# Half-size weight loads, free stage distances, full-height compressed values and unused products at the start of a two-layer hybrid decoder

## Chip, cores and metric

The kernel runs on one core of one Trainium2 chip. The metric is the device time of one execution in microseconds (us). The kernel before took 648.5 us (median of three runs, 647.51 to 649.08).

## What is computed

A trunk of two pre-norm residual layers on 256 tokens of width 1024, all in float32. In every layer four token mixers with four heads of 64 each read one normalised input through one input projection of 2956 columns. Their outputs go through one output projection, and an MLP with squared ReLU (width 4096) follows. A last RMS norm ends it. Cut to what matters:

```python
for layer in range(2):
    h = _rmsnorm(x, norm_attn[layer])
    proj = h @ w_in[layer]                       # 1024 x 2956
    o_sb = stick_breaking_attention(...)         # "sb"
    o_mb = moba_attention(...)                   # "mb", one 256-block here: causal softmax with bias
    o_ns = nsa_attention(...)                    # "ns": g0 * compressed + g1 * selected + g2 * window
    o_df = diff_attention(...)                   # "df": softmax1 - lam * softmax2, then RMS norm
    x = x + concat(o_sb, o_mb, o_ns, o_df) @ w_out[layer]
    h2 = _rmsnorm(x, norm_mlp[layer])
    x = x + square(relu(h2 @ w_up[layer])) @ w_down[layer]
return _rmsnorm(x, final_norm)
```

The compressed branch of "ns" first makes 15 compressed keys and values from windows of 32 tokens: a product of 2048 x 256 weights (w1), a GELU, and a second product (w2). With 256 tokens every selected block is causal, so the selected and the window branch have the same scores up to keys and values.

## The kernel before

**Products.** Every product with a weight is made of three, because each float32 operand is split into a rounded part (hi) and the rest (lo): hi*hi, hi*lo, lo*hi. A piece of weights is loaded by SP's queue (tile `wraw`, 1 MB, three buffers), split by ACT into `whi` (a copy that rounds) and by DVE into `wlo` (a subtraction), in halves of 0.5 MB with four buffers each, and then streamed by TensorE. `class Weights` (lines 631 to 656) holds this: `load` starts the load, `part(i)` makes the split of half i. The first group of the projection ("vg", 396 columns) has smaller pieces (792 KB).

**Stages.** The start loads x, normalises it, transposes it on TensorE into `x` (hi and lo). The projection runs group by group: "vg" (values, gates), "sqk" (queries and keys of sb), "nqk" (of ns), "dqk" (of df), "v2" (values of df and mb), "mqk" (of mb). Queries and keys are split (`qth`, `qtl`), and then restacked by loads from one place of SBUF to another (`stack2`, tile `s`; `stack3` goes through DRAM, tile `st`), which run on SP's queue too. Each head of a mixer is a unit (lines 857, 905, 960, 1068) that gives up control between its stages: scores, softmax, transposes, product with the values. `compress` (line 1004) makes the compressed keys `KC` and values `VC`, reading `wraw` straight as a moving operand with stationary tiles of 32 columns. Then follow the output projection and the MLP, which are nearly all weight products.

**What sets the order.** No engine's order is written down. Calls are recorded with a due time: `at(clock, offset)` sets it, `run` (line 848) takes a head's first due time from the table `START` and adds a constant `STAGE` of 1.2 for each further stage, `LOADS` says how long ahead of its use a piece is loaded, and `LEADS` the same for its split. `Order.schedule` (line 348) then places call after call on the five engines, always the ready one of the earliest due time whose buffers are free; `choose` (line 360) passes over calls that can't start, but on SP it stops at the first load that has no buffer. It has constants for the engines' costs (`GAP`, `DRAIN` and others). The order it makes is fixed in the program; on the chip each engine works through its own list and waits on semaphores. Loads use eight semaphores in turn, so in the program a load waits until the eighth load ahead of it has landed.

**The small set-up.** `setup_consts`, `setup_bias` and `setup_small` (lines 562 to 626) load masks, the table of the relative bias (`tb`, `hot`, `rt`; one product `ps<-t,tb` on TensorE, a trip through DRAM, and six copies to `Bt` on DVE) and small vectors. They stand between the projections of layer 0.

Of the kernel before, what the change touches and what calls it, by code (L numbers as in the profile page):

```python
# [27 lines left out]
    "sb": ((-2128.1, -135.2, -1435.8, 37.9), (-286.7, -731.7, -641.4, 39.7)),  # L28
    "ns": ((27.1, -1051.7, 53.8, 45.5), (48.2, -2101.2, 32.8, -175.5)),
    "cw": ((-1062.2,), (-2120.7,)),  # L30
    "cmp": ((-1801.8,), (-695.1,)),
    "df": ((-1887.0, -3174.2, -1854.8, -2205.7), (24.0, -2246.5, 53.7, 52.7)),
    "mb": ((-87.3, -1433.6, -45.1, -356.5), (-276.0, -1568.2, -350.0, -7140.8)),
# [9 lines left out]
)  # L43
LEADS = (
# [17 lines left out]
)  # L62
CW_LOAD = 41.5
STAGE = 1.2

FIRST = (-100.5, -617.1)
# [63 lines left out]
GAP, DRAIN = 13.0, 94.0  # L130
# [5 lines left out]
SPARE = {"ps": 2}  # L136

# [40 lines left out]
class Order:  # L178
# [169 lines left out]
    def schedule(self):  # L348
# [11 lines left out]
        def choose(e):  # L360
            skipped, pick = [], None
            while ready[e] and pick is None:
# [121 lines left out]
def trunk(ctx: ExitStack, tc: tile.TileContext, x, w_in, w_out, w_up, w_down, gattn, gains, pos, cw1, cw2,  # L484
# [50 lines left out]
    nc.sync.dma_start(gn, gains)  # L535
    for f in range(2):
# [9 lines left out]
    negone = cp.tile([128, 128], F32R, name="negone")  # L546
    nc.gpsimd.memset(F(negone), -1.0)
# [5 lines left out]
    KC = [cp.tile([128, 2, 16], F32R, name=f"KC{i}") for i in range(2)]  # L553
    w2 = cp.tile([128, DEPTH, 2, 2, 64], F32, name="w2")
# [7 lines left out]
    def setup_consts():  # L562
# [4 lines left out]
        for i in range(2):  # L567
            nc.gpsimd.tensor_copy(KC[i], Pc[:, 0, 0, :].rearrange("p (a b) -> p a b", a=2))
        for l in range(DEPTH):
# [11 lines left out]
    def setup_bias():  # L581
# [5 lines left out]
        nc.sync.dma_start(rt, rows)  # L587
        p = ps_att()
# [4 lines left out]
        nc.sync.dma_start(scr, vb[:12])  # L593
        for g in range(6):
# [6 lines left out]
            nc.vector.tensor_copy(Bt[:, 2 * g:2 * g + 2, :], rev)  # L601
        nc.gpsimd.memset(Bc, 8.0 * NEG)
# [3 lines left out]
    def setup_small():  # L606
        lv = t2()
        nc.sync.dma_start(lv[:, :DEPTH * 128], lamv.to_broadcast([128, DEPTH * 128]))
        d = small(4)
# [12 lines left out]
        sl = small(2)  # L622
        nc.sync.dma_start(sl, subln)
# [7 lines left out]
    class Weights:  # L631


        def __init__(self, src, n, parts):
            self.src, self.n, self.m, self.raw = src, n, n // parts, None
            self.k = n_piece[0]
            n_piece[0] += 1

        def load(self, clock):
            if self.raw is None:  # L640
                at(clock, -LOADS[self.k])
                self.raw = wp.tile([128, 2048], F32, name="wraw", tag="wraw", bufs=3)
                nc.sync.dma_start(self.raw[:, :self.n], self.src)
                at(clock)
            return self.raw

        def part(self, i, clock):
            self.load(clock)
# [3 lines left out]
            src = self.raw[:, i * self.m:(i + 1) * self.m]  # L652
# [78 lines left out]
    def proj(l, name, xT, tok, clock):  # L731
# [6 lines left out]
        ws = [Weights(w_in[l, :, o + i * 4 * n:o + (i + 1) * 4 * n], 4 * n, 2) for i in range(2)]  # L738
# [109 lines left out]
    def run(unit, l, name, h):  # L848
# [3 lines left out]
        for _ in unit(h):  # L852
            clock += STAGE
            at(clock)
# [149 lines left out]
    def compress(l, clock, early):  # L1004
# [4 lines left out]
        for i in range(2):  # L1009
            w = [Weights(cw1[l, kv, :, i * 2048:i * 2048 + 2048], 2048, 1) for kv in range(2)]  # L1010
            w = [a.load(early + 1.8 * i) for a in w]
            at(clock)
            for j in range(4):
                for kv in range(2):
                    for m in range(2):
                        g, ic = 32 * (2 * kv + m), 2 * j + m
                        x0 = 256 * kv + 16 * (8 * i + ic)
                        mm(acc[g:g + 32, :256], xf[:, x0:x0 + 32], w[kv][:, ic * 256:(ic + 1) * 256],
# [368 lines left out]
```

## Time and profile before

| | |
|---|---|
| median of 3 runs | 648.5 us |
| profiled execution | 648.43 us |
| its span, first to last instruction | 646.7 us |
| TensorE (PE) busy | 622.2 us, 96% |
| VectorE (DVE) busy | 441.7 us, 68% |
| ScalarE (ACT) busy | 358.9 us, 56% |
| GpSimd (POOL) busy | 8.3 us, 1% |
| moved by loads and stores | 126.94 MB, mean 196 GB/s |
| chain that ended last | PE 75%, DMA 9%, DVE 8%, ACT 5% |

All calls carry line 480, where the recorded calls are issued, so rows are told apart by tiles. In a row, `out<-in` are tiles without their numbers, `PEld` is TensorE's load of a stationary tile, `SPq` an issue on SP's queue. A matmul's time in a row reaches from its start to its modelled end, and matmuls overlap: the spacing of their starts says how fast TensorE goes. The time outside the span (648.43 less 646.7) is 1.7 us.

### The profile page before, as it was taken

The numbers are of one execution on the slowest core, as the hardware profiler recorded it, in microseconds if no ns is written. First come the engines' busy times: TensorE is split into PE (matmuls) and PEld (weight loads), VectorE is DVE, ScalarE is ACT, GpSimd is POOL, SyncE is SP. The second block draws the span as 40 slices with busy tenths as digits, with TensorE's granted clock in tenths as the row PEclk, the third lists the DMA queues.
The fourth block names the chain that finished last, engine by engine and source line by source line (L and its number), as shares of the span: only waits on it lengthen the run. The fifth ranks groups of instructions, "written<-read, shape, count | busy, mean of one in ns | idle before, by whom it ended". The sixth has DMA issues, their size and how long they took to land.

```text
span 646.7 us, 9744 instructions
## 1 busy us (share of the span) xinstructions
PE 622.2 (96%) x3674; PEld 529.0 (82%) x3674; DVE 441.7 (68%) x900; ACT 358.9 (56%) x693; POOL 8.3 (1%) x25
## 2 busy tenths in 40 slices
PE   5989999999999999999999999999999999999995
PEld 4978768788888888888889977887788888888885
DVE  5749579779576566556686674998866666576466
ACT  5547587566455454445364774776744454454453
POOL 2010000000000000000000000000000000000000
PEclk9999999999999999999999999999999999999999
DMA  7787955844354465555636958446355555545531
GB/s 275 254 246 227 273 196 222 255 148 176 122 215 155 176 256 186 199 192 196 212 112 222 276 222 235 190 126 236 127 196 195 196 199 191 197 162 196 196 130 66
DMA packets 26895, 126.94 MB, mean 196 GB/s; under 512 B 3880, under 2 KB 5928, under 8 KB 14048
## 3 DMA queue, kind: packets, MB, share of 16 engines
q1 hardware_dynamic: 26848, 126.32, 57.0%
q8 instruction: 29, 0.48, 0.3%
q14 instruction: 18, 0.15, 0.1%
HBM read 115.79 MB, written 3.17 MB: 184 GB/s over the span
## 4 chain that ended last, share of the span: by engine, by line
PE 75%; DMA 9%; DVE 8%; ACT 5%; issue 1%; SPq 1%; POOLq 0%; POOL 0%; ACTq 0%; DVEq 0%
PE ps L480 75%; DMA wraw<-in_w_in_dram 3%; DVE wlo L480 3%; DVE t L480 2%; ACT t L480 2%; ACT whi L480 2%; DMA wraw<-in_cw_dram 2%; DVE xs L480 1%; DMA cst<-in_cst_dram 1%; DMA s<-qtl 1%; DMA wraw<-in_w_down_dram 1%; DVE x L480 1%; SPq L480 1%; DMA t<-bias_scratch 1%; ACT x L480 1%
## 5 line engine op out<-in xcount | busy, mean ns | idle before, releaser
L480 DVE TENSOR_TENSOR wlo<-wraw,whi 128x1024 fp32r<-128x1024 f32 (+1 forms) x192 | 231.2, 1212 | 109.6 <-ACT whi L480 93.7
L480 ACT ACTIVATE whi<-wraw 128x1024 fp32r<-128x1024 f32 (+1 forms) x192 | 199.8, 1049 | 147.0 <-PE ps L480 111.3
L480 PE MATMUL ps<-x,whi 128*128 128x256 f32 (+1 forms) x1024 | 212.7, 341 | 0.7 <-DVE x L480 0.7
L480 PEld LDWEIGHTS ps<-x,whi 128*128 128x128 f32 x1024 | 153.8, 190 | 15.9 <-issue 1.2
L480 PE MATMUL ps<-whi,t 128*128 128x512 f32 (+1 forms) x528 | 162.6, 385 | 0.3 <-ACT whi L480 0.3
L480 PEld LDWEIGHTS ps<-x,wlo 128*128 128x128 f32 x768 | 112.9, 190 | 12.0 <-issue 0.6
L480 PE MATMUL ps<-x,wlo 128*128 128x256 f32 x768 | 122.0, 283 | 0.1
L480 PEld LDWEIGHTS ps<-whi,t 128*128 128x128 f32 x528 | 97.8, 188 | 20.1 <-ACT whi L480 1.0
L480 PE MATMUL ps<-wlo,t 128*128 128x512 f32 (+1 forms) x264 | 101.0, 385 | 0.0
L480 ACT ACTIVATE t<-ps 128x256 f32<-128x256 f32 (+1 forms) x109 | 44.1, 413 | 45.9 <-PE ps L480 45.1
L480 PEld LDWEIGHTS ps<-wlo,t 128*128 128x128 f32 x264 | 49.7, 188 | 9.5 <-DVE wlo L480 0.2
L480 ACT ACTIVATE t<-t 128x512 fp32r<-128x512 f32 (+5 forms) x53 | 29.3, 552 | 35.4 <-DVE t L480 33.6
L480 ACT ACTIVATE t<-t,sm 128x128 f32<-128x128 f32 (+1 forms) x98 | 42.2, 443 | 10.7 <-DVE sm L480 10.4
L480 DVE TENSOR_TENSOR t<-ps,t 128x256 f32<-128x256 f32 x64 | 26.7, 421 | 28.0 <-ACT t L480 27.3
L480 PE MATMUL ps<-whi,x 128*128 128x512 f32 (+1 forms) x128 | 36.0, 384 | 1.0 <-ACT x L480 1.0
L480 DVE TENSOR_TENSOR t<-t,t 128x512 fp32r<-128x512 f32 (+2 forms) x44 | 27.4, 622 | 8.0 <-ACT t L480 6.9
L480 DVE CUSTOM_DVE_ANT_0 t<-ps,Bt 128x256 f32<-128x256 f32 (+1 forms) x80 | 24.4, 352 | 9.0 <-PE ps L480 9.0
L480 PEld LDWEIGHTS ps<-whi,x 128*128 128x128 f32 x128 | 23.1, 193 | 4.7 <-ACT x L480 1.5
L480 PE MATMUL ps<-whi,mixh 128*128 128x512 f32 (+1 forms) x68 | 26.7, 397 | 0.0
L480 PE MATMUL ps<-whi,mixl 128*128 128x512 f32 (+1 forms) x68 | 26.5, 389 | 0.0
L480 PE MATMUL ps<-wlo,mixh 128*128 128x512 f32 (+1 forms) x68 | 26.3, 386 | 0.0
L480 DVE SCALAR_TENSOR_TENSOR t<-t 128x512 f32<-128x512 f32 (+1 forms) x36 | 22.9, 635 | 1.0
(139 smaller groups left out, 475.1 us busy)
## 6 DMA issues: line engine op xcount, KB each, us to landing
wraw<-in_w_up_dram SPq DMA_DIRECT2D x32, 1024.0 KB, 4.8
wraw<-in_w_down_dram SPq DMA_DIRECT2D x32, 1024.0 KB, 4.8
wraw<-in_w_in_dram SPq DMA_DIRECT2D x20, 1024.0 KB, 4.9
wraw<-in_cw_dram SPq DMA_DIRECT2D x8, 1024.0 KB, 9.4
wraw<-in_w_out_dram SPq DMA_DIRECT2D x8, 1024.0 KB, 6.6
s<-qth SPq DMA_DIRECT2D x28, 128.0 KB, 4.3
s<-qtl SPq DMA_DIRECT2D x28, 128.0 KB, 3.2
wraw<-in_w_in_dram SPq DMA_DIRECT2D x4, 792.0 KB, 6.7
```

What stands on the lines that cost most here:

```text
L480: fn(*a, **k)
```

## The change

Five things change in the code, and with them all tables of due times.

1. A piece of weights is loaded in two halves of 0.5 MB (396 KB in "vg"), each with its own tile: six buffers of 128x1024 in place of three of 128x2048, and a due time in `LOADS` for each half. `compress` takes its weights in halves too.
2. `run` takes the distance from each stage to the next out of a table `STAGES`, by mixer, layer, head and stage, in place of the constant 1.2. The set-up calls get due times of their own (`SETUP`).
3. `VC` becomes one constant tile of 128 rows by four heads; head h fills only its own 32 rows, the others stay zero. The product with the values then takes all 128 rows of `PcT`, in place of a 32-row tile of the array.
4. Forty products of a constant tile with itself, whose result nothing reads, stand ahead of the first transposes on TensorE; the tile they read is now the first that POOL fills.
5. `choose` lets SP pass over up to four loads that have no buffer; `GAP` goes from 13 to 14.

```diff
-LOADS = (
-    73.4, 61.3, 61.1, 82.6, 43.8, 72.8, 7.3, 8.2, 12.4, 12.9, 12.9, 2.7, 12.4, 54.6, 14.0, 10.8, 14.3, 8.1, 7.0,
...
+LOADS = (
+    (60.0, 60.0), (43.4, 52.4), (31.5, 52.8), (53.2, -1.0), (-1.0, 2.0), (11.9, -1.0), (-1.0, 60.0), (3.1, 7.5),
...
-STAGE = 1.2
+STAGES = {
+    "sb": (((-4.1, -139.2, -205.8, 69.1, 218.6), (-250.0, 90.5, -244.3, 66.4, -11.9), (-90.8, 226.5, -190.8,
...
-GAP, DRAIN = 13.0, 94.0
+GAP, DRAIN = 14.0, 94.0
...
+WARM = 40
...
-                    if e == "SP":
+                    if e == "SP" and len(skipped) == 4:
                         skipped.append(x)
                         break
...
+    at(-1000.0)
+    negone = cp.tile([128, 128], F32R, name="negone")
+    nc.gpsimd.memset(F(negone), -1.0)
...
+    at(-1000.0)
+    p = ps_att()
+    for i in range(WARM):
+        mm(p[:, 0:128], negone, negone, i == 0, i == WARM - 1)
+    at(-100.0)
...
+    VC = cp.tile([128, 4, 64], F32, name="VC")
+    nc.gpsimd.memset(VC, 0.0)
...
-        def load(self, clock):
-            if self.raw is None:
-                at(clock, -LOADS[self.k])
-                self.raw = wp.tile([128, 2048], F32, name="wraw", tag="wraw", bufs=3)
-                nc.sync.dma_start(self.raw[:, :self.n], self.src)
+        def load(self, i, clock):
+            if self.raw[i] is None:
+                at(clock, -LOADS[self.k][i])
+                self.raw[i] = wp.tile([128, 1024], F32, name="wraw", tag="wraw", bufs=6)
+                nc.sync.dma_start(self.raw[i][:, :self.m], self.src[:, i * self.m:(i + 1) * self.m])
...
-        for _ in unit(h):
-            clock += STAGE
+        for s, _ in enumerate(unit(h)):
+            clock += STAGES[name][l][h][s]
             at(clock)
...
-        VC = ap.tile([128, 64], F32, name="VC", tag="VC", bufs=2)
-        evac(VC, p[:, 0:64])
-        return VC, clock
+        for h in range(4):
+            r = slice(32 * h, 32 * h + 32)
+            evac(VC[r, h], p[r, 0:64])
+        return clock
...
-            av.append((VCs[0][32 * h:32 * h + 32], PcT[32 * h:32 * h + 32], 0))
+            av.append((VC[:, h], PcT, 0))
```

The order that comes out is another one almost everywhere. Three places follow.

SP's queue at the start, before: x, the first two pieces of "vg" and those of the groups behind it (`wraw_111`, `wraw_116` are "vg"; `wraw_123`, `wraw_128` "sqk"), and the small loads of the set-up behind them.

```order
L480 DMA xs_68<-in_x_dram 128x512 x2
L480 DMA ident_69<-in_eye_dram 128x128
L480 DMA gains_70<-in_gains_dram 128x24
L480 DMA xs_68<-in_x_dram 128x512 x2
L480 DMA wraw_111<-in_w_in_dram 128x1584
L480 DMA wraw_128<-in_w_in_dram 128x2048
L480 DMA wraw_116<-in_w_in_dram 128x1584
L480 DMA wraw_123<-in_w_in_dram 128x2048
L480 DMA wraw_188<-in_w_in_dram 128x2048
L480 DMA wraw_183<-in_w_in_dram 128x2048
L480 DMA wraw_298<-in_w_in_dram 128x2048
L480 DMA cst_71<-in_cst_dram 128x547
```

And with the change, from the fourth half of a weight on (all of x, `ident`, `gains` and three halves of "vg" stand ahead; `wraw_119` is the last half of "vg", `wraw_127` the first half that "sqk" needs, `wraw_130` and `wraw_133` its next two).

```order
L511 DMA wraw_130<-in_w_in_dram 128x1024
L511 DMA wraw_119<-in_w_in_dram 128x792
L511 DMA wraw_133<-in_w_in_dram 128x1024
L511 DMA tb_176<-in_table_dram 32x12
L511 DMA t2_177<-in_hot_dram 32x512
L511 DMA rt_178<-in_rows_dram 12x513
L511 DMA cst_71<-in_cst_dram 128x547
L511 DMA pst_85<-in_pos_dram 128x32
L511 DMA w2_83<-in_cw2_dram 128x256
L511 DMA wraw_217<-in_w_in_dram 128x1024
L511 DMA pst_85<-in_pos_dram 128x32
L511 DMA wraw_127<-in_w_in_dram 128x1024
```

The loads of the bias table moved ahead of the weights of the second group, and the first half of that group went behind nine other loads.

TensorE around the product of the bias table (`ps<-t,tb`), before, in the middle of the third group's products (`x_101,whi` and `x_101,wlo`):

```order
L480 MATMUL ps<-x_101,whi 128x256 x16
L480 MATMUL ps<-x_101,wlo 128x256 x8
L480 MATMUL ps<-x_101,whi 128x256 x2
L480 MATMUL ps<-t_171,tb 12x512
L480 MATMUL ps<-x_101,whi 128x256 x14
```

And with the change, where `whi,x_103` with 396 columns is "vg" and `x_103,whi` is the second group:

```order
L511 MATMUL ps<-whi,x_103 128x396 x5
L511 MATMUL ps<-wlo,x_103 128x396 x2
L511 MATMUL ps<-whi,x_103 128x396 x2
L511 MATMUL ps<-t_177,tb 12x512
L511 MATMUL ps<-x_103,whi 128x256 x16
```

It moved up by one group, to the end of "vg".

TensorE around the product of the compressed values (`PcT,VC`) in layer 0, before; `64x256` and `64x128` are the products with the values, which use half the array's columns, and `whi,mixh` is the output projection:

```order
L480 MATMUL ps<-whi,mixl 128x512
L480 MATMUL ps<-PcT,VC 64x256 x2
L480 MATMUL ps<-ident,t_270 128x128 x3
L480 MATMUL ps<-ident,t_271 128x128 x3
L480 MATMUL ps<-whi,mixh 128x512
```

And with the change, later in the same layer:

```order
L511 MATMUL ps<-t_289,Vn 64x256
L511 MATMUL ps<-t_300,Vn 64x256
L511 MATMUL ps<-t_289,Vn 64x128
L511 MATMUL ps<-t_300,Vn 64x128
L511 MATMUL ps<-PcT,VC 64x256 x2
L511 MATMUL ps<-t_327,V_318 64x256
```

The product stands among others of its own array shape.

## Rows read from the trace of the kernel before

**Rows 1.** The page, parts 1 and 2: busy time by engine, load share and GB/s in 40 slices.
```profile
PE 622.2 (96%) x3674; PEld 529.0 (82%) x3674; DVE 441.7 (68%) x900; ACT 358.9 (56%) x693; POOL 8.3 (1%) x25
DMA  7787955844354465555636958446355555545531
GB/s 275 254 246 227 273 196 222 255 148 176 122 215 155 176 256 186 199 192 196 212 112 222 276 222 235 190 126 236 127 196 195 196 199 191 197 162 196 196 130 66
```

**Rows 2.** Windows of 20 us: length, then busy PE, PEld, DVE, ACT, POOL; clock; DMA share, GB/s.
```profile
20.00:40.00 20.00, 18.98 (x149) 17.95 (x148) 11.39 (x15) 8.90 (x14) 2.57 (x6) 1.00 0.86 272
...
180.00:200.00 20.00, 20.00 (x105) 16.68 (x104) 13.31 (x17) 10.09 (x15) 0.00 (x0) 1.00 0.53 192
```

**Rows 3.** Timeline of PE at the start: start us, us, what, count, idle before and releaser.
```profile
7.41 4.17 PE L480 MATMUL ps<-ident,xn 128*128 128x128 f32 x16 [7.41 <-DVE xn L480]
...
12.97 0.86 PE L480 MATMUL ps<-whi,x 128*128 128x396 f32 x2
13.63 0.66 PE L480 MATMUL ps<-wlo,x 128*128 128x396 f32 x2
...
18.80 0.52 PE L480 MATMUL ps<-wlo,x 128*128 128x396 f32 x2
19.16 0.34 PE L480 MATMUL ps<-whi,x 128*128 128x396 f32 x1
```

**Rows 4.** Timeline of ACT and of DVE at the start, the splits of "vg".
```profile
10.21 1.62 ACT L480 ACTIVATE whi<-wraw 128x792 fp32r<-128x792 f32 x2 [1.03 <-DMA wraw<-in_w_in_dram]
...
18.16 2.11 DVE L480 TENSOR_TENSOR wlo<-wraw,whi 128x792 fp32r<-128x792 f32 x2
```

**Rows 5.** Timeline of PE, 34 to 46 us: the bias product and the first scores.
```profile
34.25 1.01 PE L480 MATMUL ps<-t,tb 32*12 32x512 f32 x2 [1.02 <-DMA t<-in_hot_dram]
...
45.52 0.68 PE L480 MATMUL ps<-s,s 128*128 128x256 f32 x4 [1.07 <-DMA s<-qtl]
```

**Rows 6.** Timeline of SP's queue: the restacking of "sb" in layer 0, first and last issues.
```profile
33.64 2.45 SPq L480 DMA_DIRECT2D s<-qth  x4
...
41.39 2.00 SPq L480 DMA_DIRECT2D s<-qtl  x2
```

**Rows 7.** Timeline of PE in layer 0: "ns" scores and compression weights.
```profile
61.74 0.47 PE L480 MATMUL ps<-nkh,s 128*128 128x512 f32 x1 [0.27 <-DMA s<-qtl]
...
71.87 1.93 PE L480 MATMUL ps<-wraw,XF 128*32 128x256 f32 x32 [0.63 <-DMA wraw<-in_cw_dram]
73.73 0.87 PE L480 MATMUL ps<-t,Vn 128*64 128x256 f32 x8
```

**Rows 8.** Timeline of PE in layer 1: scores of "sb", "ns" and "mb", compression.
```profile
361.04 1.12 PE L480 MATMUL ps<-x,wlo 128*128 128x256 f32 x8
362.00 0.57 PE L480 MATMUL ps<-s,s 128*128 128x256 f32 x4
...
372.44 0.94 PE L480 MATMUL ps<-nkh,s 128*128 128x512 f32 x4 [1.04 <-ACT t L480]
...
398.59 1.72 PE L480 MATMUL ps<-wraw,XF 128*32 128x256 f32 x28 [0.69 <-DMA wraw<-in_cw_dram]
...
438.86 0.47 PE L480 MATMUL ps<-s,s 128*128 128x256 f32 x2 [1.27 <-DMA s<-qtl]
```

**Rows 9.** Timeline of PE: two of one array shape, then a change of shape.
```profile
119.71 0.40 PE L480 MATMUL ps<-wlo,mixh 128*128 128x512 f32 x1
119.94 0.40 PE L480 MATMUL ps<-whi,mixl 128*128 128x512 f32 x1
120.27 1.52 PE L480 MATMUL ps<-t,Vn 128*64 128x256 f32 x16
```

**Rows 10.** Waits of TensorE's weight loads and of SP's queue: us in total, times, longest.
```profile
PEld ps L480 <- issue: 12.2, 36, 1.7
...
SPq L480 <- DMA wraw<-in_w_in_dram: 24.5, 8, 5.3
```

**Rows 11.** Loads from one tensor: KB each, median us from issue to landing.
```profile
wraw<-in_w_in_dram SPq DMA_DIRECT2D x20, 1024.0 KB, 4.9
```

More of the change, by code (lines that the diff above doesn't have):

```diff
@@ L27 @@
 START = {
[L28 to L33, printed above, removed]
+    "sb": ((-0.7, 25.9, -122.8, 41.4), (-194.1, -250.0, -250.0, 49.9)),
+    "ns": ((-37.7, -235.8, 48.9, 58.0), (30.4, -206.6, -244.7, -55.9)),
+    "cw": ((-190.7,), (-152.6,)),
+    "cmp": ((-250.0,), (-88.7,)),
+    "df": ((-237.0, 58.0, -160.4, -19.9), (-13.1, -250.0, -15.5, 55.4)),
+    "mb": ((-203.2, -173.7, -213.8, -92.8), (-54.6, -196.1, 57.4, 39.2)),
 }
 LOADS = (
[6 rows of a table removed]
[14 rows of a table added]
 )
 LEADS = (
[17 rows of a table removed]
-)
-CW_LOAD = 41.5
-STAGE = 1.2
-FIRST = (-100.5, -617.1)
[17 rows of a table added]
+)
+CW_LOAD = (44.9, 43.1)
+STAGES = {
[6 rows of a table added]
+    "cmp": (((-181.1, 87.8, -154.2, -52.4, -175.7),), ((-147.7, 87.8, -234.4, 11.8, 30.5),)),
[8 rows of a table added]
+}
+SETUP = (
+    -28.4, -13.0, -42.2, -1.4, -179.2, 250.0, 22.1, 0.0, -2.4,
+)
+FIRST = (-227.9, -87.0)
 LAYER = 300.0
@@ L535, in trunk @@
     nc.sync.dma_start(gn, gains)
+    at(-100.0, SETUP[8])
     for f in range(2):
         nc.sync.dma_start(xs[:, 1, f * 512:(f + 1) * 512], xv[:, 1, f * 512:(f + 1) * 512])
+    at(-100.0)
+    at(-1000.0)
+    negone = cp.tile([128, 128], F32R, name="negone")
+    nc.gpsimd.memset(F(negone), -1.0)
     at(-100.0)
@@ L545, in trunk @@
     nc.gpsimd.memset(G, 0.0)
-    negone = cp.tile([128, 128], F32R, name="negone")
-    nc.gpsimd.memset(F(negone), -1.0)
+    at(-1000.0)
+    p = ps_att()
+    for i in range(WARM):
+        mm(p[:, 0:128], negone, negone, i == 0, i == WARM - 1)
+    at(-100.0)
     tri = cp.tile([128, 128], F32R, name="tri")
@@ L560, in trunk, with setup_consts @@
     nc.gpsimd.memset(XF[:, 32], 0.0)
-    def setup_consts():
+    def setup_consts(clock):
+        at(clock, SETUP[0])
         nc.sync.dma_start(c, cst)
@@ L568, in setup_consts @@
             nc.gpsimd.tensor_copy(KC[i], Pc[:, 0, 0, :].rearrange("p (a b) -> p a b", a=2))
+        at(clock, SETUP[1])
         for l in range(DEPTH):
@@ L579, in trunk, with setup_bias @@
     gsub = cp.tile([128, DEPTH], F32, name="gsub")
-    def setup_bias():
+    def setup_bias(clock):
+        at(clock, SETUP[2])
         tb = ap.tile([32, 12], F32, name="tb")
@@ L587, in setup_bias @@
         nc.sync.dma_start(rt, rows)
+        at(clock, SETUP[3])
         p = ps_att()
@@ L593, in setup_bias @@
         nc.sync.dma_start(scr, vb[:12])
+        at(clock, SETUP[4])
         for g in range(6):
@@ L601, in setup_bias @@
             nc.vector.tensor_copy(Bt[:, 2 * g:2 * g + 2, :], rev)
+        at(clock, SETUP[5])
         nc.gpsimd.memset(Bc, 8.0 * NEG)
@@ L604, in setup_bias, with setup_small @@
         nc.vector.tensor_copy(Bc[:, 0, :, 0:7], Bt[:, 4:8, 159:256:16])
-    def setup_small():
+    def setup_small(clock):
+        at(clock, SETUP[6])
         lv = t2()
         nc.sync.dma_start(lv[:, :DEPTH * 128], lamv.to_broadcast([128, DEPTH * 128]))
+        sl = small(2)
+        nc.sync.dma_start(sl, subln)
+        at(clock, SETUP[7])
         d = small(4)
@@ L621, in setup_small @@
                                            e[:, 2 * l + 1:2 * l + 2], op0=ALU.add, op1=ALU.subtract)
-        sl = small(2)
-        nc.sync.dma_start(sl, subln)
         for l in range(DEPTH):
@@ L631, in trunk, with __init__ @@
     class Weights:
-        def __init__(self, src, n, parts):
-            self.src, self.n, self.m, self.raw = src, n, n // parts, None
+        def __init__(self, src, n):
+            self.src, self.m, self.raw = src, n // 2, [None, None]
             self.k = n_piece[0]
             n_piece[0] += 1
-        def load(self, clock):
-            if self.raw is None:
-                at(clock, -LOADS[self.k])
-                self.raw = wp.tile([128, 2048], F32, name="wraw", tag="wraw", bufs=3)
-                nc.sync.dma_start(self.raw[:, :self.n], self.src)
+        def load(self, i, clock):
[3 more added lines that the diff above has]
+                nc.sync.dma_start(self.raw[i][:, :self.m], self.src[:, i * self.m:(i + 1) * self.m])
                 at(clock)
-            return self.raw
+            return self.raw[i]
         def part(self, i, clock):
-            self.load(clock)
+            src = self.load(i, clock)[:, :self.m]
             at(clock, -LEADS[self.k][i])
@@ L737, in proj @@
         o = GOFF[name]
-        ws = [Weights(w_in[l, :, o + i * 4 * n:o + (i + 1) * 4 * n], 4 * n, 2) for i in range(2)]
+        ws = [Weights(w_in[l, :, o + i * 4 * n:o + (i + 1) * 4 * n], 4 * n) for i in range(2)]
         step = 2.6 * n / 512
@@ L1009, in compress @@
         for i in range(2):
-            w = [Weights(cw1[l, kv, :, i * 2048:i * 2048 + 2048], 2048, 1) for kv in range(2)]
-            w = [a.load(early + 1.8 * i) for a in w]
+            w = [Weights(cw1[l, kv, :, i * 2048:i * 2048 + 2048], 2048) for kv in range(2)]
+            w = [[a.load(k, early + 1.8 * i + 0.9 * k) for a in w] for k in range(2)]
             at(clock)
@@ L1151, in attention @@
         if l == 0:
-            setup_consts()
+            setup_consts(clock)
+            at(clock)
         acc, clock = proj(l, "sqk", xT, False, clock)
@@ L1160, in attention @@
         if l == 0:
-            setup_bias()
+            setup_bias(clock)
+            at(clock)
         acc, clock = proj(l, "nqk", xT, False, clock)
@@ L1168, in attention @@
         if l == 0:
-            setup_small()
+            setup_small(clock)
+            at(clock)
         acc, clock = proj(l, "dqk", xT, False, clock)
@@ L1175, in attention @@
         at(clock)
-        VC, _ = compress(l, base + START["cw"][l][0], base + CW_LOAD)
+        compress(l, base + START["cw"][l][0], base + CW_LOAD[l])
         at(clock)
-        VCs[:] = [VC]
         run(cmp, l, "cmp", 0)
@@ L1230, in out_proj @@
         for n, (name, idx) in enumerate(order):
-            w = Weights(w_out[l, idx], 2048, 2)
+            w = Weights(w_out[l, idx], 2048)
             m = mix[name].mix
@@ L1262, in up @@
             ps = [ps_att() for _ in range(2)]
-            w = Weights(w_up[l, j], 2048, 2)
+            w = Weights(w_up[l, j], 2048)
             hl = [w.part(c2, clock + 2.6 * c2) for c2 in range(2)]
@@ L1288, in down @@
         def down(j, h, clock):
-            w = Weights(w_down[l, j], 2048, 2)
+            w = Weights(w_down[l, j], 2048)
             lhs = [(h[0][:, i * 256:(i + 1) * 256], h[1][:, i * 256:(i + 1) * 256]) for i in range(2)]
@@ L1325, in trunk @@
     at(DEPTH * LAYER)
-    fn = wp.tile([128, 2048], F32, name="wraw", tag="wraw", bufs=3)
+    fn = wp.tile([128, 1024], F32, name="wraw", tag="wraw", bufs=6)
     nc.sync.dma_start(fn[:, :D], fnorm.to_broadcast([128, D]))
@@ L1331, in trunk @@
         r = rms(t)
-        o = wp.tile([128, 2048], F32, name="wraw", tag="wraw", bufs=3)
+        o = wp.tile([128, 1024], F32, name="wraw", tag="wraw", bufs=6)
         xf = xn[:, t]
```

4 lines of the change are left out of this document (1 added, 3 removed), and 65 rows, old and new, of tables (LEADS, LOADS, STAGES).

## Prediction

> **What bounds the kernel now.** I read the page first. TensorE is busy 622.2 of the 646.7 us span [rows 1], so at most 24.5 us is idle, and no other engine is near it. Next the windows, to see where that idle time lies. From 180 to 200 us, an MLP, TensorE is busy 20.00 of 20: there a change of order can win nothing, unless busy time itself shrinks. From 20 to 40 us it is busy 18.98, and there the load share is 0.86 at 272 GB/s [rows 2], against a digit of 3 to 5 over most of the rest [rows 1]. So idle time sits in the start, the tail and the mixers, and loads are tight only in the first 80 us. Then the timeline of TensorE, for what ended each gap. Seven gaps answer to things that the change moves: 1.02 us before the bias product and 1.07 before the first scores of "sb" [rows 5]; 0.27 and 0.63 at the "ns" scores and the compression of layer 0 [rows 7]; 1.04, 0.69 and 1.27 at "ns", compression and "mb" of layer 1 [rows 8]. Their sum is 5.99 us. The start is 7.41 us until the first transpose [rows 3]; the tail's order is the same in both kernels. So the most that vanishing waits can give is about 6, less what new waits take.
>
> The sum is made against the profiled execution, 648.43 us (span 646.7 and 1.7 around it); the median is 648.5, which is the same.
>
> **Start.** TensorE works at two speeds there. Two products of 396 columns are 0.66 us apart (12.97 to 13.63), which is 0.33 each, the lower level (1.2 GHz); from 18.80 to 19.16 two are 0.36 apart, 0.18 each, the upper level (2.4 GHz) [rows 3]. The page's granted clock is 1.00 in such windows and does not show it. The unused products have 128 columns, so cost 0.33 x 128/396 = 0.107 us at the lower level, 4.3 us for 40. Begun by 3.1 us they end before 7.41 and delay nothing; POOL fills their tile as its first work of the span, ahead of everything that ends there now, so they should begin in time. If they bring the upper level in time, the 16 transposes (4.17 us) and the eight slow products before 13.95 save at most half of their time: 16 x 0.107 + 8 x 0.15 = 2.9 us. But "vg" is bound by its splits: ACT has the first piece at 10.21, and DVE's last two splits of "vg" run from 18.16 to 20.27 [rows 4], about 1.05 each, the rest of TensorE's "vg" work following. A half piece lands sooner than a whole one, but ACT's third split and DVE's transposes of x still line up behind it. Bounds 0 and -2.9; I take **-0.8**, nearer to the DVE row than to the clock.
>
> **Bias product.** It waits 1.02 us for a small load [rows 5]. With the change the three loads of the table stand ahead of 13 others and the product one group later than its data: **-1.0** (-1.3 to -0.9). The bounds are that wait with and without a few tenths of its stationary load. The six copies of the bias on DVE come earlier too; DVE is not full there.
>
> **Scores of "sb", layer 0.** The wait of 1.07 us [rows 5] follows restacking loads that SP issues from 33.64 to 43.4 us, some 10 us [rows 6]. In the changed order 95 instead of 77 products of the third group lie between the second group's last product and the first scores. Eight of them take 0.96 us (361.04 to 362.00), 0.12 each [rows 8], so 18 more cover 2.2 us. But SP also has twice the weight issues there, 0.6 each from the row of 4 in 2.45 [rows 6]: three or four more would eat all of it. I take **-0.6** (-1.1 to +0.3).
>
> **"ns" and compression, layer 0.** 0.27 and 0.63 [rows 7] end with a restack and with a compression weight. In halves the first 16 products can start on 0.5 MB. **-0.7** (-0.9 to +0.5; the loss if SP's extra issues delay the restack).
>
> **Layer 1.** Scores of "sb": no wait now, the data came just in time at 362.00 [rows 8]; the cover falls from 86 products to 78, 8 x 0.12 = 0.96. **+0.7** (0 to +1.0). Scores of "ns": 47 products become 65, 18 x 0.12 = 2.2, and eight products with values, 0.87 [rows 7], come in, while a block of scores moves away; some 1.2 of cover against 1.04 of wait [rows 8]. The releaser named is ACT, perhaps for a free buffer, which more cover serves too. **-1.0** (-1.04 to 0). Compression: 0.69 [rows 8], halves, **-0.4** (-0.69 to +0.3). Scores of "mb": 28 products become 26 but one pair of value products more, some 0.4 of net cover against 1.27 [rows 8]: **-0.4** (-0.8 to +0.3).
>
> **Compressed values at 128 rows.** Two like products stand 0.23 apart (119.71 to 119.94); when the next has another array shape it is 0.33 (to 120.27) [rows 9]. So a switch costs 0.10. The order has 53 before and 41 after, as the value products of one shape now stand together: **-1.1** (-1.4 to -0.8). The count of streamed columns stays. The one fill of zeros is on POOL, busy 8.3 us in all [rows 1]; the copies of `VC` become four of 32 rows a layer instead of one, beside DVE at 68% and ACT at 56%, off the path as long as they come before the late value products: 0. If that cover is gone, three more copies like `KC`'s, some tenths each, hold one product: +0.5.
>
> **Halves of weights.** One hundred and four more loads cost SP only their issues; TensorE never waits for SP's time itself in the MLPs [rows 2]. Splits were in halves already, so ACT and DVE do the same work: 0. A half can be split when it has landed instead of with its whole piece, and a buffer is free sooner. Against it: loads use eight semaphores in turn, so at most eight are open, and open bytes halve. A piece of 1 MB takes 4.9 us at the median [rows 11], 214 GB/s alone, while 272 is moved in the windows [rows 2], so several overlap already. Weights need a mean of 196 GB/s; eight open halves (4 MB) would carry that with a landing time of up to 20 us. I take 0; the other end is a rival.
>
> The Trainium skill, "DMA: Bandwidth & Descriptors", section "Bandwidth", asks for loads of 1 MiB or more to reach 75% of peak. That speaks against this change; a sum by it, with its neighbour "SBUF — State Buffer" (the setup-cost knee) giving about 2 us fixed for each transfer, would add 104 x 2 = 208 us of queue time if loads went one by one. The 272 GB/s with loads of 4.9 us shows that they do not go one by one, so it adds nothing to my sum.
>
> **Stage distances.** Within busy time TensorE's weight loads wait 12.2 us, in 36 places, for nothing the profile shows [rows 10]. A new order may drop or make such places. **-0.7** (-4 to +3).
>
> **Sum.** -0.8 -1.0 -0.6 -0.7 +0.7 -1.0 -0.4 -0.4 -1.1 -0.7 = -6.0, so 648.4 - 6.0 = **642.4 us**. The single bounds added are -14 and +6; ends seldom meet, so about -3.5 and -8 hold this case.
>
> **Rivals.**
> *The larger gain.* The table of distances also removes places where TensorE is slowed within its busy time. For: 12.2 us of weight-load waits [rows 10], up to 4 of it. Against: nothing names their cause, and the MLPs are full. 642.4 - 4 = 638.
>
> *Waits change places.* Layer 1's "sb" scores lose 0.96 of cover and come out 1 us late; other gaps of about 1 us open where the order is tight, as the old order has seven. The waits on restacked data hang on SP's queue and its landings, not on when TensorE is due. Only the switches' 1.1 is left: 647.5.
>
> *The loads become the bound, slower.* SP has twice the loads with only eight open. The first place is `wraw_127`, the first half of "sqk": it is the 21st load and waits for the 13th, behind small loads. Ahead of it lie x (1 MB), all of "vg", three halves and the set-up, about 4.7 MB; 275 GB/s over the first 16 us is 4.4 MB [rows 1], so it lands near 18 to 19, and its splits (about 1 us on ACT) are ready at 19.5 to 20.5. TensorE needs it when "vg" ends, at 20.5 to 21. So it decides from a lateness of about 1 us. Then TensorE pays one hold like those of SP's queue behind weights, 24.5/8 = 3.1 us [rows 10], and one of some 1.2 us, like the "mb" wait [rows 8], at each of six places: four projection groups and two compressions. 642.4 + 3.1 + 7.2 = 652.7. Against it: SP's holds are on average in stretches with a load share of 3 to 5 [rows 1]; the tight stretch is 80 us long.
>
> *That it doesn't do what it says:* the unused products may leave the clock as it was; that takes only part of 0.8 away and stays inside the forecast.
>
> **Numbers.** The forecast, 641 to 645: 0.50. The larger gain, about 638: 0.17. Waits change places, 647.5: 0.13. Slower, about 653: 0.20. The range leaves out the far half of the slower case and the far quarter of the larger gain: 636.5 to 651. A measurement tells 0.2%, 1.3 us, from no change. Faster than 647.2: the forecast, the larger gain and half of the third case: 0.73. Same: the rest of the third: 0.07. Slower than 649.8: 0.20.
>
> **What would show it.** Right: 40 products end before the first transpose, and two of 396 columns stand 0.18 apart from the first; no idle time before the bias product; the "ns" wait in layer 1 gone and a new one below 1 us near the first "sb" scores there; value products in longer runs; TensorE at 20.00 of 20 in the MLP windows. Wrong: TensorE idle for weights (released by `whi` or `wlo`) at group changes or in an MLP; SP waiting much over 24.5 us on weights with TensorE waiting behind it; TensorE's busy time (622.2, less 1 to 2 for clock and switches, plus 4.3 unused) changed by more than 3 us either way.

## Result and the profile of the changed kernel

The changed kernel takes **673.6 us** (median of 4 runs, 672.0 to 676.1) against 648.1 of the kernel before (4 runs, 647.5 to 649.1). The ratio is 1.0395, with a 95% interval from 1.0359 to 1.0432: 4% **slower**, where 642.4 was forecast. The range ended at 651. One execution each of two kernels below lay far off, 3465.6 us in e8_after_price and 2146.8 in e12_slots_all_no_unused, and their medians are given without it.

The page of the changed kernel, its busy time on TensorE and its granted clock in 40 slices, against [rows 1]:

```profile
span 674.1 us, 10128 instructions
PE 638.7 (95%) x3714; PEld 540.6 (80%) x3714; DVE 437.5 (65%) x892; ACT 361.5 (54%) x707; POOL 10.2 (2%) x26
PEclk9999998999998999999999998999999998999999
```

The span grew by 27.4 us: 10.9 more idle time (674.1 - 638.7 = 35.4, before 24.5) and 16.5 more busy time. The added busy time is not useful work: 8.8 of it are the unused products, and most of the rest is the clock. The mean granted clock is 0.988 (0.999 before), so 0.012 x 674.1 = 8.1 us of full speed are lost, 0.6 before. The unused products stand where TensorE was idle: before its first product it idles 1.0 us instead of 7.4, so behind that its idle time grew by 17.3 us (34.4 against 17.1).

Where it lies is told by the times at which TensorE starts the transposes at each boundary (`xn` into a mixer stage, `xs` into an MLP) and its last product, from the timelines of the two kernels:

| us | until the first transpose | mixers, layer 0 | MLP, layer 0 | mixers, layer 1 | MLP, layer 1 |
|---|---|---|---|---|---|
| before | 7.4 | 135.0 | 184.0 | 129.6 | 183.9 |
| changed | 9.6 | 135.7 | 194.5 | 136.0 | 191.4 |
| difference | +2.2 | +0.7 | **+10.6** | **+6.4** | **+7.5** |

So 18.1 of 27.4 us were lost in the MLPs, where [rows 2] have TensorE at 20.00 of 20 and where I had expected nothing. Of these, 9.1 are idle time of TensorE that ends with a split of weights (`whi` 6.1, `wlo` 3.0; 0.3 in the whole kernel before), and 3.4 are two falls of the clock, shown below. The rest lies within what the profile counts as busy, and no row tells it apart. Windows of the changed kernel, same columns as [rows 2]; the second and fourth are in the MLPs:

```profile
20.00:40.00 20.00, 19.73 (x151) 18.41 (x149) 12.50 (x21) 9.68 (x14) 2.00 (x2) 1.00 0.95 312
200.00:220.00 20.00, 17.96 (x78) 13.98 (x78) 9.74 (x11) 8.09 (x11) 0.00 (x0) 0.91 0.48 156
400.00:420.00 20.00, 15.05 (x122) 9.68 (x121) 5.41 (x15) 6.33 (x18) 0.00 (x0) 0.91 0.82 224
540.00:560.00 20.00, 17.96 (x78) 14.44 (x77) 9.71 (x12) 8.93 (x12) 0.00 (x0) 0.91 0.41 141
```

In an MLP window TensorE does 78 products instead of some 105, idles 2 us, and the load share is 0.48: the DMA engines are half idle while TensorE waits for weights. What holds it there? The timelines of TensorE, ACT and SP's queue:

```profile
209.89 0.50 PE L511 MATMUL ps<-whi,t 128*128 128x512 f32 x1 [1.03 <-ACT whi L511]
211.15 0.62 PE L511 MATMUL ps<-wlo,t 128*128 128x512 f32 x1 [0.76 <-DVE wlo L511]
...
201.56 2.01 ACT L511 ACTIVATE whi<-wraw 128x1024 fp32r<-128x1024 f32 x2 [4.13 <-DMA wraw<-in_w_up_dram]
208.78 1.06 ACT L511 ACTIVATE whi<-wraw 128x1024 fp32r<-128x1024 f32 x1 [4.70 <-DMA wraw<-in_w_down_dram]
...
195.43 0.33 SPq L511 DMA_DIRECT2D wraw<-in_w_up_dram  x1
203.90 0.33 SPq L511 DMA_DIRECT2D wraw<-in_w_down_dram  x1
```

TensorE waits at 209 us for a split that begins at 208.78, when its half has landed; that half was issued at 203.90; and between 195.43 and 203.90 SP issued nothing. Joining the loads of the program with the trace shows why (us; issue ended, split began, buffer free when the second split ended):

```
half        from     issued   split    free
wraw_593    w_down   172.69   220.48   222.97
wraw_575    w_down   175.58   210.01   212.57
wraw_565    w_up     192.35   202.52   205.01
wraw_580    w_up     193.49   210.96   213.70
wraw_647    w_down   194.63   258.48   260.96
wraw_562    w_up     195.76   201.56   203.87
wraw_572    w_down   204.23   208.78   211.10
```

Six halves fill the six buffers at 195.76. Two of them are not split for another 25 and 63 us (`wraw_593`, `wraw_647`). The next half needed, `wraw_572`, has no buffer until `wraw_562` has been split at 203.87, and is issued at once. Its split begins at 208.78, 4.6 us after the issue ended, so load, split, TensorE and the next load stand in one row. The chain of waits has that row again and again in the second MLP (here from 486 to 555 us), load, split, split, load:

```profile
489.12 6.50 DMA wraw<-in_w_up_dram
495.66 0.04 issue
495.71 1.07 ACT whi L511
496.80 1.23 DVE wlo L511
498.02 0.03 DVE t L511
498.05 3.72 DMA wraw<-in_w_down_dram
```

Of the 128 halves of the MLPs 49 are split within 6 us of their issue and 34 more than 20 us after it; of the 64 whole pieces before, 35 and 2. So a split soon after the load is nothing new; new are the halves loaded far ahead, which hold buffers all that time.

Behind such a wait the clock can fall as well. Windows around it, and around another fall, at 102 us; the number before the last two is the granted clock:

```profile
98.00:102.00 4.00, 3.71 (x31) 3.42 (x30) 3.90 (x11) 2.92 (x10) 0.00 (x0) 1.00 0.68 243
102.00:105.50 3.50, 3.50 (x19) 2.56 (x18) 3.13 (x17) 2.53 (x10) 0.00 (x0) 0.52 0.53 177
...
203.00:211.40 8.40, 6.55 (x34) 5.02 (x33) 4.14 (x6) 3.70 (x6) 0.00 (x0) 1.00 0.39 125
211.40:214.80 3.40, 3.40 (x9) 2.62 (x9) 3.33 (x5) 0.88 (x3) 0.00 (x0) 0.50 0.70 236
214.80:218.00 3.20, 3.20 (x15) 2.63 (x15) 1.92 (x2) 1.58 (x2) 0.00 (x0) 1.00 0.70 218
```

Behind a stretch with 1.85 us of idle time TensorE goes at 1.2 GHz and does 9 products in 3.4 us; then 15 in 3.2 at 2.4 GHz. There are four such stretches of about 3.4 us (from 102, 211, 416 and 556 us), and each costs 1.7 us, 6.8 in all. Three stand behind waits for weights. The one from 102 us does not: in the 10 us before it no wait is over 0.32 us, and TensorE had just done twelve products of only 32 columns among longer ones. Why the clock fell there is not shown.

### The profile page after: what moved, and what is told of

It is laid out like the page before. It is cut to its first block, busy times and chain, and to the rows that moved or that the text cites. A ratio compares the mean times of both kernels' runs of the same rounds, so it can differ in the third digit from the quotient of the medians.

```text
span 674.1 us, 10128 instructions
## 1 busy us (share of the span) xinstructions
PE 638.7 (95%) x3714; PEld 540.6 (80%) x3714; DVE 437.5 (65%) x892; ACT 361.5 (54%) x707; POOL 10.2 (2%) x26
## 5 line engine op out<-in xcount | busy, mean ns | idle before, releaser
L511 ACT ACTIVATE whi<-wraw 128x1024 fp32r<-128x1024 f32 (+1 forms) x192 | 197.7, 1049 | 185.1 <-DMA wraw<-in_w_up_dram 57.2
L511 PE MATMUL ps<-whi,t 128*128 128x512 f32 (+1 forms) x528 | 167.4, 390 | 4.5 <-ACT whi L511 4.5
L511 PEld LDWEIGHTS ps<-whi,t 128*128 128x128 f32 x528 | 99.4, 191 | 26.1 <-ACT whi L511 6.8
L511 PE MATMUL ps<-wlo,t 128*128 128x512 f32 (+1 forms) x264 | 103.2, 392 | 3.0 <-DVE wlo L511 3.0
L511 ACT ACTIVATE t<-ps 128x256 f32<-128x256 f32 (+2 forms) x110 | 44.2, 411 | 29.6 <-PE ps L511 28.9
L511 ACT ACTIVATE t<-t,sm 128x128 f32<-128x128 f32 (+1 forms) x102 | 43.8, 443 | 17.3 <-DVE sm L511 17.1
L511 PE MATMUL ps<-whi,x 128*128 128x512 f32 (+1 forms) x128 | 35.4, 383 | 0.3 <-ACT x L511 0.3
```

The lines of the kernel that those rows point to most:

```text
L511: fn(*a, **k)
```

## Experiments

"Order kept" means that the planner works as in the kernel named, with its buffers, and only what it hands out at the end is changed. Theory A says that halves come late because of when they are loaded, B that the new order of the computing engines is itself worse, C that halves are dear by themselves; A was split further as runs came in.

**Is it the loads at all?** The calls that load pieces are left out, and every reader of a piece reads one tile filled once:

```diff
+                if op.bytes and op.writes[0].tensor.name in self.pieces:
+                    continue
-                fn(*a, **k)
+                fn(*[kept(v) for v in a], **{n: kept(v) for n, v in k.items()})
```

> The changed kernel with its order on TensorE, VectorE and ScalarE kept, but no piece of weights is loaded: every split and every compression product reads one tile that is filled once at the start (so the output is that of constant weights). Theory A, halves come late: the 25 us are time in which TensorE waits for halves, and time at the lower clock behind such waits; without loads the time falls to 640 to 648. Theory B, the order on the computing engines is itself worse (chains of the mixers, shape switches, unused products): 665 or more stays. Theory C, each half load is dear by itself: as A here.

> The same for the kernel before: its order kept, no piece of weights loaded, all splits read one constant tile. Theory A: TensorE was hardly held by loads before, so 641 to 647, a fall of 1 to 7 us, most of it at the start and the two compression waits (0.63 and 0.69). Under theory B the difference between this run and the changed kernel without loads stays near 25 us; under A it is within 5.

Measured: 639.1 for the changed kernel (ratio 0.985, 0.984 to 0.987), 642.3 for the kernel before (0.990, 0.989 to 0.992). Loads cost the changed kernel 673.6 - 639.1 = **34.5 us**, the kernel before 6.1. Theory B is out: without loads the changed order is 3.2 us the better one, in spite of its unused products. Not all of that is a gain of the order: 2.5 us lie in layer 1's MLP (183.3 us against 185.8), which takes 183.9 in the kernel before with its loads. The mixers take 3.1 us less (127.1 and 126.0 against 129.8 and 126.4), the start 2.5 more. The window of the changed order that had 15.05 us of work, now without loads:

```profile
400.00:420.00 20.00, 19.98 (x152) 18.09 (x152) 19.52 (x76) 17.95 (x53) 0.00 (x0) 1.00 0.01 2
```

**Are halves dear by themselves?** The old order, each piece by two loads:

```diff
+                    for i in range(2):
+                        fn(a[0][:, i * n // 2:(i + 1) * n // 2], a[1][:, i * n // 2:(i + 1) * n // 2])
+                    continue
```

> The kernel before with its order and buffers kept, each piece of weights brought by two loads of half the columns, one behind the other, instead of one. Theory A: the number of loads does no harm, since the old order has whole pieces of slack; 646 to 650. Theory C, twice the loads are dear by themselves (SP issues, packets of half the size): 655 or more.

Measured: 652.9 (648.9 to 659.3 in ten runs), ratio 1.0076 (1.0045 to 1.0107). Between the two expectations: halves cost some 5 us in the old order, all of it in layer 1's mixers (134.8 us against 129.6), none in the MLPs (183.7 and 183.7). The place, TensorE at the "ns" scores and the windows around it:

```profile
372.88 1.62 PE L486 MATMUL ps<-nkh,s 128*128 128x512 f32 x4 [2.59 <-ACT XF L486]
...
362.00:372.70 10.70, 8.28 (x64) 7.85 (x63) 8.77 (x17) 10.28 (x21) 0.00 (x0) 1.00 1.02 288
372.70:379.50 6.80, 6.62 (x20) 3.15 (x21) 1.29 (x9) 1.95 (x9) 0.00 (x0) 0.50 0.05 20
```

TensorE came 1 us earlier than before and waited to nearly the same moment (372.9; 372.4 in [rows 8]), with a load share of 1.02; then it went 6.8 us at the lower clock, which costs 3.4. So more than half of the loss in this profile is the clock's. C falls, as 655 or more was stated for it, and halves by themselves do not explain the 18 us of the MLPs.

**The unused products alone.** In the kernel before:

```diff
+            for i in range(40):
+                tc.nc.tensor.matmul(p[:, 0:128], t, t, start=i == 0, stop=i == 39, skip_group_check=True)
```

> The kernel before with only the forty unused products ahead of the first transposes, nothing else moved. If they raise the clock for the first products and splits bind the first group: 0 to -1; if TensorE binds it: down to -2.9 (645.6). If they delay the first transposes: up to +4.

Measured: 649.7 (646.5 to 651.1), ratio 1.0014 (0.9999 to 1.0028): no gain, and by the trace a loss of 1.0 us at the start. The start of TensorE's timeline there:

```profile
0.99 8.80 PE L481 MATMUL ps<-unused 128*128 128x128 f32 x40 [0.99 <-POOL unused L479]
9.59 2.95 PE L484 MATMUL ps<-ident,xn 128*128 128x128 f32 x16
12.29 0.61 PE L484 MATMUL ps<-whi,x 128*128 128x396 f32 x2
```

Each takes 0.22 us, not the 0.107 that I had worked out from 396 columns, so they end at 9.59 and hold the transposes for 2.2 us. The transposes then take 2.7 us instead of 3.8, as the last five of them start 0.11 us apart and the others 0.21; and the second group begins at 22.33 instead of 21.32.

**Does order of use heal it?** SP's loads sorted by first use, each issued as soon as a buffer is free, the computing engines' order kept:

```diff
+            while sync >= 6 and free and k < len(first) and first[k] in loads:
+                out.append(loads[first[k]])
+                free, k = free - 1, k + 1
```

> The changed kernel with its order on the three computing engines and all its halves kept; only SP's loads of halves are put in the order in which the splits use them, each as soon as one of the six buffers is free. Theory A1, halves loaded 20 to 64 us ahead hold buffers, so that the urgent ones are loaded one after the other as each split ends: the 34 us that loads cost in this kernel go nearly all, 640 to 648. Theory A2, a half load is simply too slow (twice the loads, each with its own time to land) whatever the order: 660 or more. Theory B is out by the run without loads.

> The same on the kernel before: its order and its three buffers of whole pieces kept, the loads of pieces in the order of use. Its loads cost 6.1 us in all (run without loads). A1: there is little to win, 644 to 649. If whole pieces in order of use hold up restacking loads on SP's queue: up to 655.

> As e5_after_by_use, without the forty unused products. They ended at 9.6 us where the first transposes had begun at 7.4 before, so without them the first group ends 1 us earlier if TensorE binds it: 1 us less than e5_after_by_use. If the clock rises later without them: up to 1 us more.

Measured: 692.6, 677.4 and 689.4 (ratios 1.071, 1.047, 1.062). By its total A2 (660 or more) would hold in e5_after_by_use, and e6_before_by_use, 22 above the highest I had allowed, is a miss. (e7_by_use_no_unused lies 3 below e5_after_by_use where 1 was expected, but its runs spread from 681.7 to 691.8.) The stages tell another thing: in e5_after_by_use the MLPs take 183.5 and 183.3 us, as good as before, and the mixers 150.3 and 155.0 (151.8 and 141.4 in e6_before_by_use). Two windows, then TensorE and SP's queue in the mixers:

```profile
40.00:60.00 20.00, 11.66 (x71) 11.48 (x72) 6.94 (x8) 3.73 (x5) 0.00 (x0) 0.80 0.91 210
...
200.00:220.00 20.00, 20.00 (x102) 16.96 (x101) 12.37 (x15) 9.93 (x13) 0.00 (x0) 1.00 0.58 184
...
56.49 1.09 PE L537 MATMUL ps<-s,s 128*128 128x256 f32 x4 [6.02 <-issue]
...
35.84 2.50 SPq L537 DMA_DIRECT2D s<-qth  x4
42.30 0.35 SPq L537 DMA_DIRECT2D wraw<-in_w_in_dram  x1
42.75 0.46 SPq L537 DMA_DIRECT2D s<-qth  x1
```

A half that SP may issue early waits at the head of the queue for a buffer, here until 42.30 (the split that frees one ends at 42.27), and the restacking loads behind it wait with it; the first scores start at 56.49 instead of 48.64. So in the mixers a load must not be early on the queue. In the MLPs, where next to nothing else is on it, loads in order of use and as early as possible heal the loss; which of the two does it, the next runs tell.

**Same places, other halves.** Every load keeps its place on SP's queue; which half it brings is sorted by use, for the MLPs' halves alone (e9, and e11 without unused products) or for all (e10, and e12 without):

```diff
+        for i, op in zip(at, sorted((done[i] for i in at), key=lambda op: use[op.writes[0].tensor.name])):
+            new[i] = op
```

> The changed kernel; on SP's queue every load keeps its place and the computing engines their order, only which half of the MLPs' weights (up and down) is loaded at which of these places is sorted by use. With loads in order of use at the earliest moment the MLP stages took 183.4 us each, against 194.6 and 191.4 in the changed kernel, while the mixers lost 33 us. Theory A1, halves far ahead of their use hold the buffers in the MLPs: the MLPs gain 15 to 19, the mixers stay, so 654 to 660. Theory A4, what healed the MLPs there was that loads were issued earlier, not their order: 668 or more.

> The same for all halves, those of the mixers too. If order of use also cures the mixers (the compression halves of layer 1, one of which comes 3.95 us late): 646 to 654. If in the mixers the places on the queue beside the restacking loads decide: as e9_after_slots_mlp or up to 8 above it.

> As e9_after_slots_mlp without the forty unused products. They run until 9.6 us, 2.2 past the start of the first transposes before, and bring the rise of the clock from 13.9 to 13.4 only: 0.5 to 2.2 us less than e9_after_slots_mlp.

> All halves sorted by use on the queue places of the changed kernel, and no unused products: e10_after_slots_all (655.5) less what the unused products cost, which was 6 between e9_after_slots_mlp (657.6) and e11_slots_mlp_no_unused (651.4) though the start alone gives 2.2: 648 to 653.

Measured: **657.6** (ratio 1.0138, 1.009 to 1.0186), 655.5 (1.0107, 1.006 to 1.0155), 651.4 (1.0046, 1.0023 to 1.0068) and 653.1 (1.0075, 1.0051 to 1.010). Sorting the MLPs' halves gives back 16.0 of the 25.5 us, and nothing but the order of the loads was touched: theory A1 holds there and A4 falls. The MLPs take 183.5 and 183.3 us, as they do without any loads (183.6 and 183.3 in e1_after_noload). The MLP windows of e9_after_slots_mlp, and its longest wait:

```profile
200.00:220.00 20.00, 20.00 (x102) 16.95 (x101) 13.74 (x16) 10.62 (x14) 0.00 (x0) 1.00 0.59 195
540.00:560.00 20.00, 20.00 (x105) 17.01 (x104) 12.96 (x16) 9.56 (x13) 0.00 (x0) 1.00 0.69 229
...
401.36 1.08 PE L525 MATMUL ps<-wraw,XF 128*32 128x256 f32 x8 [4.05 <-DMA wraw<-in_cw_dram]
```

Now no half of an MLP is split within 6 us of its issue; the median is 13.7 us. Sorting the mixers' halves too takes that last wait away, but 655.5 and 657.6 can't be told apart. The unused products cost 6.2 us by one pair (e9, e11), where 0.5 to 2.2 was expected, and 2.4 by the other (e10, e12); the start alone shows 2.5 (first transpose at 9.6 or at 7.1). The runs of one kernel spread over 6 us here, and the longer ones have the lower mean clock (e10_after_slots_all: 652.6 us at 0.994, 658.4 at 0.985, which is worth 5.9 us). So I hold to the 2.5.

**Is it the planner's price of a load?** One constant of the planner raised, a new order made from the same due times:

```diff
-DMA_START, DMA_SEEN, DMA_RATE = 625.0, 908.0, 360.0
+DMA_START, DMA_SEEN, DMA_RATE = 625.0, 2500.0, 360.0
```

> The changed kernel with its tables and one constant of the planner raised: a load lands 2.5 instead of 0.9 us after its data (0.5 MB: 4.6 us from its issue instead of 3.0, as the trace has it). The planner then makes another order of all engines with the same due times. Theory A3, the price alone is at fault: 650 or less. A1 (due times put halves far ahead of their use, which a price does not change): 655 or more.

Measured: 684.7 (ratio 1.059, 1.054 to 1.063). A3 falls as stated: the price alone mends nothing, and 33 halves of the MLPs are still split more than 20 us after their issue (34 in the changed kernel). It does not say that the price was right; due times made for the higher price weren't tried. Nor does a run part what in the planner puts halves so far ahead: their due times, or the four loads that `choose` may now pass over.

**What is left, in layer 1's mixers.** A restacking load goes ahead of halves that are due later:

```diff
+                if piece(a) and not piece(b) and due(a) > max(begun(b) + 6000, (due(b) if due(b) < 1e9 else 0.0) + 3000):
+                    new[i:j + 1] = new[i + 1:j + 1] + [a]
```

> As e12_slots_all_no_unused, and on SP's queue a restacking load goes ahead of a half that is due later than it (over 3 us after its first use, and over 6 after the restack can begin). Theory A5, the rest of the loss, in layer 1's mixers (about 6 us), is restacking loads that come late behind and among halves: 642 to 648, and the waits on restacked tiles (3.02, 1.42, 1.31 us with all halves sorted) shrink. Theory A6, these land late because of the load on the DMA engines, whatever the place: no less than e12_slots_all_no_unused.

Measured: 662.5 (ratio 1.0221), 9 above e12_slots_all_no_unused. A5 falls in this form. TensorE's two longest waits in it:

```profile
88.25 2.79 PE L539 MATMUL ps<-st 96*128 96x256 f32 x12 [7.27 <-DMA st<-parts_scratch]
...
415.68 1.51 PE L539 MATMUL ps<-st 96*128 96x256 f32 x6 [5.60 <-DMA wraw<-in_w_out_dram]
```

In e12_slots_all_no_unused layer 0's mixers take 132.7 us, 2.3 less than before, both MLPs 183.5 and 183.3, and layer 1's mixers 138.9, 9.3 more. Its windows there and its two longest waits:

```profile
400.00:404.00 4.00, 2.23 (x14) 1.63 (x13) 2.58 (x5) 1.79 (x6) 0.00 (x0) 1.00 1.04 249
404.00:411.00 7.00, 6.82 (x28) 6.46 (x29) 4.01 (x23) 3.83 (x16) 0.00 (x0) 0.51 0.89 356
...
404.18 1.51 PE L527 MATMUL ps<-st 96*128 96x256 f32 x6 [1.95 <-DMA st<-parts_scratch]
...
444.81 0.59 PE L527 MATMUL ps<-s,s 128*128 128x256 f32 x2 [2.89 <-DMA s<-qth]
```

The DMA engines are full (1.04) when the restacked tile is late, and TensorE then goes at the lower clock (0.51 over 404 to 411, 28 products in 7 us). That speaks for A6, but no run took load off the engines there without taking the loads away, so it isn't shown. No complete version beat the kernel before.

## Why the prediction was wrong

By its own steps, with what each term measured in the changed kernel. TensorE's waits in its mixers, against [rows 5, 7, 8]:

```profile
22.20 1.02 PE L511 MATMUL ps<-t,tb 32*12 32x512 f32 x2
...
41.03 1.22 PE L511 MATMUL ps<-x,wlo 128*128 128x256 f32 x8 [1.30 <-DVE wlo L511]
...
48.64 0.68 PE L511 MATMUL ps<-s,s 128*128 128x256 f32 x4 [0.75 <-DMA s<-qtl]
...
65.55 1.18 PE L511 MATMUL ps<-wraw,XF 128*32 128x256 f32 x16 [0.29 <-DVE sm L511]
...
85.22 1.60 PE L511 MATMUL ps<-st 96*128 96x256 f32 x12 [0.89 <-DMA st<-parts_scratch]
...
127.22 1.45 PE L511 MATMUL ps<-s,s 128*128 128x256 f32 x11 [1.61 <-DMA s<-qtl]
...
390.24 0.47 PE L511 MATMUL ps<-nkh,s 128*128 128x512 f32 x1 [1.10 <-DMA s<-qtl]
...
415.86 1.67 PE L511 MATMUL ps<-wraw,XF 128*32 128x256 f32 x16 [3.95 <-DMA wraw<-in_cw_dram]
...
460.15 0.50 PE L511 MATMUL ps<-s,s 128*128 128x256 f32 x2 [1.74 <-DMA s<-qtl]
```

- **"Halves of weights ... I take 0": this step failed**, and with it the sentence that in the MLPs "a change of order can win nothing". It can lose there. The step costed the loads (issues, open bytes, landing) and never asked in which order they bring the halves. Both were there to be read: the order of SP's queue is fixed in the program, and the diff has the six buffers, each held from its load to the second of its two splits (`whi`, `wlo`). Price: 18.1 us in the MLPs, 16.0 of the total given back by sorting their loads (e9_after_slots_mlp). A sign of being wrong that the prediction named, TensorE idle for `whi` or `wlo` in an MLP, is what the rows show.
- **"The loads become the bound, slower"** had the sign (chance 0.20) and not the place or the size. Its first place, `wraw_127`, was harmless: the first group, with the bias product behind it, ends at 23.2, and no wait stands there. Its price per wait, 1.2 to 3.1 us, left out that the clock can fall behind a wait, 1.7 us in each of three places.
- **Half a piece lands hardly sooner.** I counted on "a half can be split when it has landed". In the MLPs halves land 4.3 and 4.7 us after their issue at the median, whole pieces 4.8 (the fastest 3.5 and 4.7): half the bytes, nearly the same time. So loads in one row bring little more than half as much per turn. The Trainium skill, "SBUF — State Buffer", section "The DMA setup-cost knee", says that a fixed time of about 2 us does not scale with the bytes; the trace agrees in direction, as half the bytes take 1.2 us off the fastest load. By its fit a half would take 2 + 524/436 = 3.2 us (an estimate from that page), which is less than the 4.3 measured beside other loads.
- **Start, -0.8**: wrong in sign. 40 x 0.22 = 8.8 us, not 4.3; the first transpose moved from 7.41 to 9.59. The price was carried over from 396 columns to 128 by proportion, though [rows 3] had a warning: the first 16 transposes, of 128 columns, take 4.17 us, 0.26 each. Whether the splits bind "vg" as I wrote is not shown: of the 2.2 us by which the transposes come later, e4_before_unused has 1.0 left at the second group.
- **Bias product, -1.0**: right. No idle time stands before it now.
- **"sb" of layer 0, -0.6**: 1.07 became 0.75, half of it. **"ns" and compression of layer 0, -0.7**: 0.90 became 0.29, right; but the `st` tile (0.89), "mb" (1.61) and a split in the third group (1.30) are new waits, +3.8.
- **Layer 1.** "sb" has no new wait (forecast +0.7). "ns" stays at 1.10 (forecast -1.0). Compression goes from 0.69 to 0.74 + 0.26 + 3.95 (forecast -0.4): its eight halves too were loaded out of order of use, the last one issued at 406.9 and wanted at 411.9; with the mixers' halves sorted these waits are gone (e10_after_slots_all). "mb" goes from 1.27 to 1.74 (forecast -0.4).
- **Array shapes and stage distances, -1.1 and -0.7**: not measured one by one. Without loads the changed mixers take 3.1 us less, where all terms but the start's add up to -5.2 with loads. That has the sign of the forecast and some half of its size, and it doesn't tell the terms apart. So the mechanisms on TensorE may have been right in part; the bound they met was not.
- **The sum's upper end.** The single upper bounds add up to +3.7 (0 -0.9 +0.3 +0.5 +1.0 +0 +0.3 +0.3 -0.8 +3), not +6. The upper end of the range, 651, came from the rivals and not from it.

## What to carry to other kernels

When a pool of buffers is cut into smaller pieces and the loads get free due times, compare the order of the loads with the order of their use before anything else: a piece loaded far ahead takes a buffer out of the pool until it is used, and with the rest held so, load, split and compute stand in one row even with the DMA engines half idle. A queue that carries both weight loads and small urgent ones has the opposite need: there a load must not be put ahead of its buffer, because it blocks what stands behind it (e5_after_by_use, e6_before_by_use). Cost a late load on TensorE at more than its wait, since the clock may fall behind it.

## What was not expected of the hardware

- A load of 512 KB lands 4.3 to 4.7 us after its issue and one of 1024 KB 4.8 (medians in the MLPs of the two kernels), while the fastest take 3.5 and 4.7.
- At the lower clock TensorE's products with 128 moving columns are 0.21 us apart and those with 396 columns 0.33, nowhere near in proportion; at the upper clock 0.11 and 0.18 (e4_before_unused, [rows 3]).
- Forty such products from 0.99 to 9.59 us did not bring the upper clock during that time. With them its spacing begins at 11.7 us in e4_before_unused and at about 13.5 in the changed kernel. Without them it begins at 14.0 in the kernel before and is there at 12.67 in e12_slots_all_no_unused, while e11_slots_mlp_no_unused still has 0.33 until 15.04. So these runs do not show that the products bring it sooner.
- The clock fell to 0.50 for some 3.4 us in four places of the changed kernel, three of them behind late loads: over 211.4 to 214.8 us behind a stretch with 1.85 us idle. It does not fall behind every wait: the windows of 20 us around the waits of 1.04 and 1.27 us in [rows 8] have it at 1.00, and so has the changed kernel around those of 1.61 (124 to 132 us) and 1.74 us (457 to 464). And it fell at 102 us with no wait over 0.32 us before.
